# Three fifths of a feed-forward's first layer with the activations stationary and 512 weight columns streaming

## The chip, the cores and the metric

The kernel runs on one core of one Trainium2 chip. The metric is the device time of one execution in microseconds. Before the change three runs took 2414.76, 2416.9 and 2419.35 us, median 2416.9.

## The reference

One block of a transformer on 256 tokens of width 2048, in float32: a feed-forward, a mixer (differential attention and a gated delta rule side by side) and a second feed-forward. Each is modulated by vectors that come from a conditioning vector c (adaLN: shift, scale and gate), and each ends in a residual sum and a layer norm. Cut to what matters here:

```python
def swiglu_ffn(h, w_in, w_out):               # w_in 2048 x 11264, w_out 5632 x 2048
    g, u = jnp.split(h @ w_in, 2, axis=-1)
    return (jax.nn.silu(g) * u) @ w_out

ada = (silu(c) @ w_ada + b_ada).reshape(B, 3, 3, D_MODEL)
shift, scale, gate = ada[:, :, 0, None], ada[:, :, 1, None], ada[:, :, 2, None]
y = swiglu_ffn(x * (1 + scale[:, 0]) + shift[:, 0], w_ffn_in[0], w_ffn_out[0])
x = layer_norm(ALPHA * x + 0.5 * gate[:, 0] * y, ...)
y = hybrid_mixer(x * (1 + scale[:, 1]) + shift[:, 1], ...)
x = layer_norm(ALPHA * x + gate[:, 1] * y, ...)
y = swiglu_ffn(x * (1 + scale[:, 2]) + shift[:, 2], w_ffn_in[1], w_ffn_out[1])
x = layer_norm(ALPHA * x + 0.5 * gate[:, 2] * y, ...)
```

## The kernel before, in words

Products are made to float32 precision in a float32r format: each operand is split into a rounded part hi and a rest lo, and `mm3` (lines 145 to 150) sums three products, hi x hi, hi x lo and lo x hi, into one PSUM bank. Each is one matmul instruction with its own weight load (a 128 x 128 stationary operand) and a moving operand of 256 or 512 columns.

Weights come from DRAM as chunks of 128 x 1024 floats, 512 KB each, in one long `plan` (lines 1464 to 1500) that fixes their order. `weights()` (lines 219 to 231) hands out the next chunk; up to six raw chunks are under way (pool `rawp`, tile `raw`), and up to four are split ahead (pool `wp`, tiles `hi` and `lo`): ACT copies raw to hi, DVE subtracts hi from raw to give lo (POOL does it in a few stretches). DMAs are issued from SP's queue.

There are two ways to use a chunk. `_wstat` (line 274) has the weights stationary: 128 weight columns at a time, with the activations' 256 tokens as the moving operand; the result has features on partitions, tokens along the row. `_xstat` (line 287) has the activations stationary: 128 tokens (t = 0 or 1) by 128 features, with 512 weight columns moving; the result has tokens on partitions. The activations come as hi and lo too: `h` (tiles `h_hi`, `h_lo`, 16 k-tiles of 128 x 256) for a sub-block's input, `hid` for the hidden layer. `h` lies in the pool `pp`, which is opened first, so that `rawp`, `wp` and the pools of each sub-block (`hid` among them) come behind it in SBUF.

A feed-forward has 44 "pairs": 128 gate columns and the 128 up columns that go with them. It runs in two halves (`SIZES`: 28 and 16 pairs in the first feed-forward, 22 and 22 in the last), each with its first layer and then its part of the second layer, since the hidden tiles of all pairs would not fit. In the first layer (lines 791 to 793) each pair is one `_wstat` over 4 chunks, 96 products of 256 columns into one bank; `_ffn_hid_run` (line 737) then makes the hidden tile: Silu on ACT, a product on DVE, and the split into hid hi (ACT) and hid lo (DVE). The first 28 pairs of the whole kernel are another way of this: they wait for the conditioning (tile `mms`, weights `w_first`) and are not touched by the change. The second layer (`_y_blocks`, line 702) is four `_xstat` with hid stationary, one per 512 output columns. The last one of a sub-block works with halves of 256 columns in its last part, so that the layer norm can start early.

At the end of the mixer, `_Next.rest` (line 569) makes the next sub-block's h: PE transposes the normed x (tile `lnt`), DVE applies scale and shift (`hf`), ACT and POOL split it. While these tiles come out, PE already works on the first two pairs of the next stage (tile `pre`).

The order of the instructions on each engine is written out by the kernel itself. `_Kernel` keeps a planned time `k.t` that grows by each product's columns; side work (hidden tiles, adaLN vectors, attention heads) runs as generator threads, and `pump()` after each `mm3` issues the next step of those whose planned time has come. `bank()` gives PSUM banks from a ring of four and waits for the thread that reads the oldest. `k.tr` is a PE transpose (line 158). The adaLN vectors are dot products on DVE (`_ada_dot`, tile `ar`) or, for gates, sums over chunks (tile `acc`) closed by two small PE products (`aps`).

The mixer has one stage with h stationary and 512 columns moving: the attention's values (`dv`, `_xstat` at line 1344, 192 products, tile `mx`). Its other projections are `_wstat`.

Of the kernel before, what the change touches and what calls it, by code (L numbers as in the profile page):

```python
# [8 lines left out]
F32 = mybir.dt.float32  # L9
F32R = mybir.dt.float32r  # L10
I32 = mybir.dt.int32
AF = mybir.ActivationFunctionType
# [6 lines left out]
S = 256  # L19
DFF = 5632  # L20
# [7 lines left out]
NEG = -1.0e30  # L28
BLK = 16
LEVELS = (128 // BLK).bit_length() - 1  # L30
SIZES = {0: (28, 16), 2: (22, 22)}
VISITS = ((0, 2, 0, 28), (2, 2, 0, 28), (4, 4, 0, 28), (8, 4, 0, 12), (8, 8, 12, 28), (12, 4, 0, 12))
SRAW = 4
FIRST_LOADS = (0, 1)
# [22 lines left out]
class _Thread:  # L57
# [3 lines left out]
    def __init__(self, k, gen):  # L61
        self.k, self.gen, self.ready, self.done = k, gen, k.t, False
# [29 lines left out]
class _Kernel:  # L92
# [118 lines left out]
    def hold(self, first, n):  # L211

        u = self.uid()
        bufs = [self.pp.tile([128, KT, S], F32R, tag=f"h_{x}", name=f"held_{x}{u}").rearrange("p a b -> p (a b)")
                for x in ("hi", "lo")]
        for i in range(n):
            self.held[first + i] = [b[:, i * 1024:(i + 1) * 1024] for b in bufs]
# [65 lines left out]
def _tile(part, kt):  # L283
    return part[kt] if isinstance(part, dict) else part[:, kt, :]


def _xstat(k, n, act, done, tail=0):

    pss = [k.bank([128, 512], "mx") for _ in range(2)]
    halves = [(0, 512)]
    pss = [[ps] for ps in pss]
    if tail:
        halves = [(0, 256), (256, 512)]
        pss = [[pss[0][0], pss[1][0]],
               [k.pss.tile([128, 512], F32, tag="sm", name=f"mx{k.uid()}") for _ in range(2)]]

    def part(c, w, j, t, i):  # L300
        kt = 2 * c + j
        act.need(k, kt)
        lo, hi = halves[i]
        sl = slice(j * 512 + lo, j * 512 + hi)
        tk = slice(t * 128, (t + 1) * 128)
        k.mm3(pss[t][i][:, lo:hi], (_tile(act[0], kt)[:, tk], _tile(act[1], kt)[:, tk]), (w[0][:, sl], w[1][:, sl]),
              start=(kt == 0), stop=(kt == 2 * n - 1))
        k.pump()

    more = max(0, tail - WB)  # L310
    if more:
        k.hold(k.nu + n - tail, more)
    for c in range(n - tail):
        w = k.weights()
        for j in range(2):
            for t in range(2):
                for i in range(len(halves)):
                    part(c, w, j, t, i)
    if not tail:
        for t in range(2):  # L320
            k.read(done(t, pss[t][0], 0, 512), 2 - t)
        return
    ws = [k.weights(max(0, i - more)) for i in range(tail)]
    for t in range(2):
        for i, (lo, hi) in enumerate(halves):
            for c in range(n - tail, n):
                for j in range(2):
                    part(c, ws[c - n + tail], j, t, i)
            for _ in done(t, pss[t][i], lo, hi):
                pass  # L330
# [154 lines left out]

def _new_h(k):
    u = k.uid()
    h = _H([k.pp.tile([128, KT, S], F32R, tag=f"h_{x}", name=f"h_{x}{u}") for x in ("hi", "lo")])
    h.ready = 0
    return h  # L490

# [53 lines left out]
class _Next:  # L545


    def __init__(self, k, idx, prep):
        self.k, self.idx, self.prep = k, idx, prep

    def step(self, stage, ada, ln):
        k = self.k
# [16 lines left out]
    def rest(self, ln):  # L569
        k, A, B = self.k, self.A, self.B  # L570
        h = _new_h(k)
        x, lnp = k.x, k.lnp
        k.xd = k.drp.tile([128, 2, D], F32, tag="xd", name=f"xd{self.idx}")

        def turn(ps, g, t):
            for j in range(2):
                f = 2 * g + j
                k.tr(ps[:, j, t * 128:(t + 1) * 128], x[t][:, f * 128:(f + 1) * 128])

        def bank(g):  # L580
            ps = k.pss.tile([128, 2, 256], F32, tag="sm", name=f"lnt{k.uid()}")
            turn(ps, g, 0)
            return ps

        ln.norm(0, 2)
        ln.norm(0, 3)
        pss = [bank(g) for g in range(3)]
        ln.factors(1)
        ln.norm(1, 0)
        k.pool_lo = 0  # L590
        def run():
            for g in range(8):
                ps = pss.pop(0)
                turn(ps, g, 1)
                for i in range(2):
                    f = 2 * g + i
                    _h_tile(k, lnp, h, f, ps[:, i, :], A[:, f:f + 1], B[:, f:f + 1])
                if g in (0, 2, 4):
                    ln.norm(1, 1 + g // 2)
                h.ready = 2 * g + 2  # L600
                h.when[2 * g] = h.when[2 * g + 1] = k.chain
                yield 0.0
                if g < 5:
                    pss.append(bank(g + 3))
            for t in range(2):
                k.nc.sync.dma_start(k.xd[:, t, :], x[t])

        th = k.spawn(run())
        th.step()
        acts = [h, h]  # L610
        pre = [k.bank([128, 2, S], "pre") for _ in range(2)]
        for c in range(4):
            for ps in pre:
                _products(k, ps, k.weights(), 4 * c, 4, acts, c == 0, c == 3)
        k.wait(lambda: th.done)
        return h, pre
# [140 lines left out]
    k.V.tensor_tensor(hid[1][j], hf, hid[0][j].bitcast(F32), ALU.subtract)  # L757


def _ffn(k, a, h, sub, items, interval, start, pre, finish, tail):  # L760

    tc = k.tc
    acts = [h, h]
    ln = _Ln(k)
    with ExitStack() as fs:
        k.hp = hp = fs.enter_context(tc.tile_pool(name=f"hid{sub}", bufs=1))
        for half, size in enumerate(SIZES[sub]):
            hid = _H([{}, {}])
            hid.ready = size
            j0 = 0  # L770
            if half == 0:

                def side():
                    k.pss = k.pss or k.ctx.enter_context(tc.tile_pool(name="pss", bufs=4, space=PSUM))
                    ada = _Ada(k, a, fs.enter_context(tc.tile_pool(name=f"ada{sub}", bufs=1)), items, interval)
                    k.lnp = fs.enter_context(tc.tile_pool(name=f"ln{sub}", bufs=1))
                    k.spawn(_load_x(k, a, k.lnp, k.lnp, ("x0", "x1"), *((1, 40.0, X_PACE) if sub else (None, 0.0, 3.0))))
                    return ada

                if start is not None:  # L780
                    j0 = size
                    ada = start(h, hid, side)
                    k.spawn(_rel_bias(k, a))
                    k.spawn(_lambda(k, a))
                    k.spawn(k.consts())
                else:
                    j0 = len(pre)
                    for j in range(j0):
                        _ffn_hid(k, pre[j], hid, j, back=j0 - j)
                    ada = side()  # L790
            for j in range(j0, size):
                ps = _wstat(k, 4, acts)
                _ffn_hid(k, ps, hid, j)
            res = _y_blocks(k, size // 2, hid, ada, sub, half == 0, ln if half else None, finish, tail)
        return res

# [636 lines left out]
def tile_hybrid_block(ctx: ExitStack, tc: tile.TileContext, names, aps):  # L1433
# [6 lines left out]
    k.pp = pp = ctx.enter_context(tc.tile_pool(name="pp", bufs=1))  # L1440
    k.rawp = ctx.enter_context(tc.tile_pool(name="rawp", bufs=RAWB))
    k.wp = ctx.enter_context(tc.tile_pool(name="wp", bufs=WB))
    k.smallp = ctx.enter_context(tc.tile_pool(name="smallp", bufs=2))
    k.drp = ctx.enter_context(tc.tile_pool(name="drp", bufs=1, space=DRAM))

# [11 lines left out]
    k.ones = pp.tile([128, 128], F32R, tag="ones", name="ones")  # L1457
    k.V.tensor_copy(k.ones, one)
    k.V.tensor_scalar(k.badaT[:, 0, 1, :], k.badaT[:, 0, 1, :], 1.0, None, ALU.add)
    k.eps = pp.tile([128, 1], F32, tag="eps", name="eps")  # L1460
    k.V.memset(k.eps, LN_EPS)
    k.xd = a["x"]

# [2 lines left out]
    plan += [a["w_first"][i] for i in range(4 * SIZES[0][0])]  # L1466
    for sub in range(2):
        j0 = 0
        if sub == 1:
            plan += [a["w_ffn_in"][sub, j, c] for c in range(4) for j in range(2)]  # L1470
            j0 = 2
        for half, size in enumerate(SIZES[2 * sub]):
            if sub or half:
                plan += [a["w_ffn_in"][sub, j, c] for j in range(j0, NPAIR if half else size) for c in range(4)]
            j0 = SIZES[2 * sub][0]
            plan += [a[f"w_ffn_out{sub}{half}"][n, c] for n in range(4) for c in range(size // 2)]
        if sub == 0:
            n0 = len(plan)
# [92 lines left out]
        d = {**ada.dst, **k.more.dst}  # L1571
        return _affine(k, 2, 1, d[(2, 0)], d[(2, 1)])

    h, pre = _ffn(k, a, h, 0, FFN_ADA, FFN_PACE, start, None, _Next(k, 0, prep0), TAIL)
    h, pre = _mixer(k, a, h, pre, lambda pool: _Ada(k, a, pool, TAIL_ADA, TAIL_PACE), _Next(k, 1, prep1))
    last = _Last(k, a, out)
    k.spawn(last.load())
    _ffn(k, a, h, 2, [(2, 2)], 6.0, None, pre, last, LAST_TAIL)
# [37 lines left out]
def _layout(inputs, np):  # L1616
# [32 lines left out]
    r["ln_gT"] = r["ln_g"].reshape(3, KT, 128).transpose(2, 0, 1)  # L1649
    r["ln_bT"] = r["ln_b"].reshape(3, KT, 128).transpose(2, 0, 1)  # L1650
    wi = g["w_ffn_in"].reshape(2, D, 2 * DFF)
    wi = [pair(w[:, :DFF], w[:, DFF:]) for w in wi]
    r["w_ffn_in"] = np.stack([chunks_w(w, 2) for w in wi])
    first = []
    for kt0, n, ja, jb in VISITS:
        m, q = min(n, 4), max(1, 4 // n)
# [49 lines left out]
```

## Time and profile before

| | |
|---|---|
| median of three runs | 2416.9 us |
| the profiled execution | 2417.43 us, of which the span is 2415.6 |
| PE (matmul) busy | 2331.5 us, 97% |
| DVE busy | 1708.3 us, 71% |
| ACT busy | 1036.6 us, 43% |
| POOL busy | 323.1 us, 13% |
| DMA | 582.06 MB, mean 241 GB/s |
| granted TensorE clock, mean | 0.984 of full speed |

PE's matmuls are pipelined: a row's duration is longer than the distance from one start to the next, so a busy share of 97% does not say how fast the products follow each other. That is to be had from the number of products in a stretch that holds nothing else. PEld is the weight load, which runs beside the products. Where a helper issues all of an engine's work, every row has the helper's line (L88), and the tiles' names tell the groups apart: out<-in.

### The profile page before, as it was taken

How to read it: one execution, taken by the hardware profiler on the slowest of the kernel's cores; microseconds unless marked ns; L12 is line 12 of the kernel's file. 1: busy time of each engine (PE TensorE's matmuls, PEld its weight loads, DVE VectorE, ACT ScalarE, POOL GpSimd, SP SyncE). 2: the span in 40 equal slices, each digit the busy share in tenths (PEclk: the TensorE clock that was granted, in tenths of full speed). 3: DMA queues.
4: the chain of work that ended last, by engine and by line, in shares of the span. 5: the costliest groups of instructions: out<-in, count | busy, mean ns of one | idle time of the engine just before them, and what ended most of it. 6: DMA issues, size and time to landing. Idle time of an engine off the chain costs nothing.

```text
span 2415.6 us, 42349 instructions
## 1 busy us (share of the span) xinstructions
PE 2331.5 (97%) x16989; PEld 2214.6 (92%) x16989; DVE 1708.3 (71%) x2538; ACT 1036.6 (43%) x1420; POOL 323.1 (13%) x218
## 2 busy tenths in 40 slices
PE   6999999999999899999999999999999999999997
PEld 6999997889998879998999999988999989999987
DVE  4767888787765687869887887876787555444456
ACT  4434444444444444444444344435434434444432
POOL 5884000000002210000000300022040000000001
PEclk8999999999999999999999999999999999999999
DMA  9997878898875565544547888876888555555553
GB/s 363 333 329 289 296 248 275 317 336 301 300 262 191 183 206 193 168 166 153 168 160 262 299 308 291 290 261 214 300 311 261 188 192 192 183 183 183 186 191 106
DMA packets 166381, 582.06 MB, mean 241 GB/s; under 512 B 19820, under 2 KB 22812, under 8 KB 165416
## 3 DMA queue, kind: packets, MB, share of 16 engines
q1 hardware_dynamic: 166184, 579.36, 68.9%
q8 instruction: 133, 2.18, 0.4%
q14 instruction: 64, 0.52, 0.1%
HBM read 572.98 MB, written 7.88 MB: 240 GB/s over the span
## 4 chain that ended last, share of the span: by engine, by line
PE 87%; DVE 7%; issue 2%; ACT 1%; DMA 1%; POOL 1%; DVEq 0%; SPq 0%; ACTq 0%; POOLq 0%
PE mm L147 15%; PE mm L148 15%; PE mm L149 15%; PE mx L149 8%; PE mx L147 8%; PE mx L148 8%; PE mms L148 4%; PE mms L147 4%; PE mms L149 4%; DVE lo L88 2%; DVE acc L88 1%; PE UY L153 1%; DVE x L88 1%; ACT hi L88 1%; PE pre L148 1%
## 5 line engine op out<-in xcount | busy, mean ns | idle before, releaser
L88 ACT ACTIVATE hi<-raw 128x1024 fp32r<-128x1024 f32 x769 | 811.9, 1059 | 995.9 <-PE mm L148 413.4
L88 DVE TENSOR_TENSOR lo<-raw,hi 128x1024 fp32r<-128x1024 f32 x690 | 855.2, 1245 | 524.6 <-ACT hi L88 516.8
L147 PE MATMUL mm<-h_hi,hi 128*128 128x256 f32 x3072 | 878.1, 286 | 0.0
L149 PE MATMUL mm<-h_hi,lo 128*128 128x256 f32 x3072 | 868.0, 283 | 3.6 <-DVE lo L88 3.6
L148 PE MATMUL mm<-h_lo,hi 128*128 128x256 f32 x3072 | 869.6, 283 | 0.0
L149 PEld LDWEIGHTS mm<-h_hi,lo 128*128 128x128 f32 x3072 | 583.3, 190 | 4.3 <-DVE lo L88 4.3
L147 PEld LDWEIGHTS mm<-h_hi,hi 128*128 128x128 f32 x3072 | 581.6, 189 | 1.9 <-issue 1.6
L148 PEld LDWEIGHTS mm<-h_lo,hi 128*128 128x128 f32 x3072 | 581.6, 189 | 1.0 <-issue 0.6
L88 POOL TENSOR_TENSOR lo<-raw,hi 128x1024 fp32r<-128x1024 f32 x79 | 189.9, 2412 | 793.4 <-ACT hi L88 793.4
L147 PE MATMUL mx<-hi,hid 128*128 128x512 f32 (+1 forms) x772 | 285.3, 370 | 1.4 <-ACT hi L88 1.4
L148 PE MATMUL mx<-lo,hid 128*128 128x512 f32 (+1 forms) x772 | 285.3, 370 | 0.8 <-DVE lo L88 0.8
L149 PE MATMUL mx<-hi,hid 128*128 128x512 f32 (+1 forms) x772 | 285.1, 369 | 0.0
L147 PE MATMUL mms<-h_hi,hi 128*128 128x256 f32 x896 | 256.2, 286 | 9.9 <-ACT hi L88 5.7
L148 PE MATMUL mms<-h_lo,hi 128*128 128x256 f32 x896 | 255.4, 285 | 3.7 <-POOL h_lo L88 3.7
L149 PE MATMUL mms<-h_hi,lo 128*128 128x256 f32 x896 | 254.3, 284 | 1.6 <-POOL lo L88 1.6
L147 PEld LDWEIGHTS mms<-h_hi,hi 128*128 128x128 f32 x896 | 170.5, 190 | 10.6 <-ACT hi L88 5.8
L148 PEld LDWEIGHTS mms<-h_lo,hi 128*128 128x128 f32 x896 | 171.3, 191 | 4.3 <-POOL h_lo L88 4.2
L149 PEld LDWEIGHTS mms<-h_hi,lo 128*128 128x128 f32 x896 | 172.1, 192 | 1.9 <-POOL lo L88 1.9
L147 PEld LDWEIGHTS mx<-hi,hid 128*128 128x128 f32 x772 | 145.5, 189 | 26.7 <-ACT hi L88 1.9
L148 PEld LDWEIGHTS mx<-lo,hid 128*128 128x128 f32 x772 | 145.5, 188 | 25.9 <-DVE lo L88 1.4
L149 PEld LDWEIGHTS mx<-hi,hid 128*128 128x128 f32 x772 | 145.5, 188 | 24.4
L88 DVE SCALAR_TENSOR_TENSOR acc<-ar,cs,acc 128x512 f32<-128x512 f32 x180 | 147.7, 821 | 6.3 <-DMA ar<-in_w_gate_dram 2.9
(295 smaller groups left out, 2436.7 us busy)
## 6 DMA issues: line engine op xcount, KB each, us to landing
raw<-in_w_ffn_in_dram SPq DMA_DIRECT2D x240, 512.0 KB, 4.4
raw<-in_w_ffn_out_dram SPq DMA_DIRECT2D x176, 512.0 KB, 4.1
raw<-in_w_first_dram SPq DMA_DIRECT2D x112, 512.0 KB, 5.1
ar<-in_w_gate_dram SPq DMA_DIRECT2D x96, 512.0 KB, 4.9
ar<-in_w_ada_dram SPq DMA_DIRECT2D x96, 512.0 KB, 5.4
sar<-in_w_ada_dram SPq DMA_DIRECT2D x64, 512.0 KB, 4.7
raw<-in_w_gab_dram SPq DMA_DIRECT2D x64, 512.0 KB, 4.7
raw<-in_w_kq_dram SPq DMA_DIRECT2D x32, 512.0 KB, 3.2
```

Of the source, the lines that this page charges most:

```text
L88: return f(*args, **kw)
L147: mm(ps, lhsT=lhs[0], rhs=rhs[0], start=start, stop=False, skip_group_check=True)
L148: mm(ps, lhsT=lhs[0], rhs=rhs[1], start=False, stop=False, skip_group_check=True)
L149: mm(ps, lhsT=lhs[1], rhs=rhs[0], start=False, stop=stop, skip_group_check=True)
L153: self.nc.tensor.matmul(ps, lhsT=lhsT, rhs=rhs, start=start, stop=stop, skip_group_check=True)
```

## The change

60 of the 88 pairs, the second half of the first feed-forward (16) and all of the last one (44), are made in blocks of four by `_ffn_block`: first the four pairs' 512 gate columns with `_xstat` (h stationary, 8 chunks, 96 products of 512 columns into two banks, one per 128 tokens), then their 512 up columns likewise into two other banks. ACT takes Silu of each gate bank into `sg0` and `sg1`, DVE multiplies by the up bank in place. As tokens now lie on partitions, a thread `turn` transposes the 2 x 4 tiles on PE into two PSUM tiles (`hT`), four transposes each, and ACT and DVE split from there into hid hi and lo. The turn starts 2 us of planned time behind DVE's planned end, and the next block's gate may be read only when it is done. `w_ffn_in` is laid out as `_xstat` wants it, and the plan asks for a block's 8 gate chunks and then its 8 up chunks. The last feed-forward's halves become 24 and 20 pairs. At its start, PE works on the first block's gate columns while h comes out (`wide`), k-tile by k-tile for both token halves, instead of on two pairs. h moves from `pp` to a pool of its own, `htp`, opened behind `rawp` and `wp`; `eps`, a tile of one float per partition that stood ahead of h, becomes 16 floats wide.

```diff
-SIZES = {0: (28, 16), 2: (22, 22)}
+SIZES = {0: (28, 16), 2: (24, 20)}
...
-    h = _H([k.pp.tile([128, KT, S], F32R, tag=f"h_{x}", name=f"h_{x}{u}") for x in ("hi", "lo")])
+    h = _H([k.htp.tile([128, KT, S], F32R, tag=f"h_{x}", name=f"h_{x}{u}") for x in ("hi", "lo")])
...
+def _xprod(k, ps, w, act, kt, j, t, lo, hi, last):
+
+    act.need(k, kt)
+    sl = slice(j * 512 + lo, j * 512 + hi)
+    tk = slice(t * 128, (t + 1) * 128)
+    k.mm3(ps[:, lo:hi], (_tile(act[0], kt)[:, tk], _tile(act[1], kt)[:, tk]), (w[0][:, sl], w[1][:, sl]),
+          start=(kt == 0), stop=(kt == last))
+    k.pump()
...
+        if self.wide:
+            pre = [k.bank([128, 512], "pre") for _ in range(2)]
+            for c in range(8):
+                w = k.weights()
+                for j in range(2):
+                    for t in range(2):
+                        _xprod(k, pre[t], w, h, 2 * c + j, j, t, 0, 512, KT - 1)
+            k.wait(lambda: th.done)
+            return h, pre
...
+def _ffn_block(k, h, hid, b, before, pre):
+    sg = {}
+
+    def gate(t, ps, lo, hi):
+        yield 0.2
+        while not all(th.done for th in before):
+            yield 0.3
+        sg[t] = k.hp.tile([128, 512], F32, tag=f"sg{t}", name=f"sg{k.uid()}")
+        k.A.activation(sg[t], ps, AF.Silu)
+
+    def up(t, ps, lo, hi):
+        yield 0.2
+        k.V.tensor_tensor(sg[t], sg[t], ps, ALU.mult)
+
+    def turn(ups):
+        while not all(th.done for th in ups):
+            yield 0.3
+        yield max(0.0, k.V.t - k.t) + 2.0
+        for g in range(2):
+            ps = k.pss.tile([128, 2, S], F32, tag="sm", name=f"hT{k.uid()}")
+            for q in range(2):
+                for t in range(2):
+                    f = 2 * g + q
+                    k.tr(ps[:, q, t * 128:(t + 1) * 128], sg[t][:, f * 128:(f + 1) * 128])
+            yield
+            js = [4 * b + 2 * g + q for q in range(2)]
+            for q, j in enumerate(js):
+                both = k.hp.tile([128, 2, S], F32R, tag=f"hid{j}", name=f"hid{k.uid()}")
+                hid[0][j], hid[1][j] = both[:, 0, :], both[:, 1, :]
+                k.A.activation(hid[0][j], ps[:, q, :], AF.Copy)
+            yield
+            for q, j in enumerate(js):
+                k.V.tensor_tensor(hid[1][j], ps[:, q, :], hid[0][j].bitcast(F32), ALU.subtract)
+
+    if pre is None:
+        _xstat(k, KT // 2, h, gate)
+    else:
+        for t in range(2):
+            k.read(gate(t, pre[t], 0, 512), 2 - t)
+    _xstat(k, KT // 2, h, up)
+    th = k.spawn(turn(list(k.users[-2:])))
+    for i in range(4):
+        hid.job(4 * b + i, th)
+    return th
...
-                    j0 = len(pre)
-                    for j in range(j0):
-                        _ffn_hid(k, pre[j], hid, j, back=j0 - j)
                     ada = side()
-            for j in range(j0, size):
-                ps = _wstat(k, 4, acts)
-                _ffn_hid(k, ps, hid, j)
+            turned = []
+            for b in range(b0, size // 4):
+                turned = [_ffn_block(k, h, hid, b, turned, None if b or half else pre)]
...
     k.rawp = ctx.enter_context(tc.tile_pool(name="rawp", bufs=RAWB))
     k.wp = ctx.enter_context(tc.tile_pool(name="wp", bufs=WB))
+    k.htp = ctx.enter_context(tc.tile_pool(name="htp", bufs=1))
...
-    k.eps = pp.tile([128, 1], F32, tag="eps", name="eps")
+    k.eps = pp.tile([128, 16], F32, tag="eps", name="eps")[:, 0:1]
...
-                plan += [a["w_ffn_in"][sub, j, c] for j in range(j0, NPAIR if half else size) for c in range(4)]
+                plan += [a[f"w_ffn_in{sub}"][i, b, c] for b in range(j0, j0 + size // 4) for i in range(2)
+                         for c in range(KT // 2)]
```

## Rows read from the trace of the kernel before

**Rows 1.** The page's part 1: busy time, share of the span, instructions.
```profile
PE 2331.5 (97%) x16989; PEld 2214.6 (92%) x16989; DVE 1708.3 (71%) x2538; ACT 1036.6 (43%) x1420; POOL 323.1 (13%) x218
```
**Rows 2.** The page's part 4: the chain that ended last, by engine, by line.
```profile
PE 87%; DVE 7%; issue 2%; ACT 1%; DMA 1%; POOL 1%; DVEq 0%; SPq 0%; ACTq 0%; POOLq 0%
PE mm L147 15%; PE mm L148 15%; PE mm L149 15%; PE mx L149 8%; PE mx L147 8%; PE mx L148 8%; PE mms L148 4%; PE mms L147 4%; PE mms L149 4%; DVE lo L88 2%; DVE acc L88 1%; PE UY L153 1%; DVE x L88 1%; ACT hi L88 1%; PE pre L148 1%
```
**Rows 3.** Busy time by windows: first-layer stages (16 and 22 pairs), then a second layer.
```profile
core 0: us, PE busy (x) PEld busy (x) DVE busy (x) ACT busy (x) POOL busy (x), PEclk, DMA share, GB/s
520.40:704.70 184.30, 184.30 (x1538) 184.30 (x1537) 140.71 (x181) 78.61 (x95) 0.00 (x0) 1.00 0.88 305
...
2025.30:2278.80 253.50, 253.50 (x2114) 253.46 (x2113) 124.38 (x134) 105.43 (x130) 0.00 (x0) 1.00 0.53 183
...
1905.60:2025.30 119.70, 119.70 (x530) 99.13 (x529) 62.10 (x58) 47.27 (x46) 0.00 (x0) 1.00 0.57 193
```
**Rows 4.** Tile mx: weight loads and products, duration min/median/max, stationary hid and h.
```profile
L148 PEld LDWEIGHTS mx<-lo,hid x772: 186/188/192, 360.8 to 2399.9; 128*128 128x128 f32 x193
L148 PE MATMUL mx<-lo,hid x772: 282/389/506, 361.0 to 2400.0; 128*128 128x512 f32 x157, 128*128 128x256 f32 x36
...
L147 PE MATMUL mx<-hi,h_hi x64: 391/398/741, 848.5 to 902.4; 128*128 128x512 f32 x64
L148 PEld LDWEIGHTS mx<-lo,h_hi x64: 187/188/192, 848.5 to 902.4; 128*128 128x128 f32 x64
L148 PE MATMUL mx<-lo,h_hi x64: 392/397/400, 848.8 to 902.6; 128*128 128x512 f32 x64
```
**Rows 5.** PE's timeline, dv products: first and last of 20 (start, duration in us).
```profile
883.01 0.40 PE L148 MATMUL mx<-lo,h_hi 128*128 128x512 f32 x1
...
887.47 0.40 PE L149 MATMUL mx<-hi,h_lo 128*128 128x512 f32 x1
```
**Rows 6.** PE's timeline: four transposes among 256-column and among 512-column products.
```profile
968.49 0.60 PE L158 MATMUL oT<-ident,kn 128*128 128x128 f32 x4
968.85 0.36 PE L147 MATMUL mm<-h_hi,hi 128*128 128x256 f32 x1
969.05 0.28 PE L148 MATMUL mm<-h_lo,hi 128*128 128x256 f32 x1
...
876.35 0.60 PE L158 MATMUL knT<-ident,kn 128*128 128x128 f32 x4
876.70 0.48 PE L147 MATMUL mx<-hi,h_hi 128*128 128x512 f32 x1
877.02 0.40 PE L148 MATMUL mx<-lo,h_hi 128*128 128x512 f32 x1
```
**Rows 7.** Groups by tile, 520 to 705 us: busy us, mean ns | idle before.
```profile
L88 DVE TENSOR_TENSOR lo<-raw,hi 128x1024 fp32r<-128x1024 f32 x65 | 79.6, 1226 | 43.6 <-ACT hi L88 41.4 <-DMA raw<-in_w_ffn_in_dram 1.5
L88 ACT ACTIVATE hi<-raw 128x1024 fp32r<-128x1024 f32 x65 | 69.0, 1061 | 107.3 <-PE mm L148 87.9 <-issue 14.1 <-DVE ada L88 1.8
L88 DVE CUSTOM_DVE_ANT_0 ar<-ar,crow,tmp 128x1024 f32<-128x1024 f32 x21 | 26.9, 1280 | 0.0
...
L88 DVE TENSOR_TENSOR hid<-hidf,hid 128x256 fp32r<-128x256 f32 x15 | 6.3, 420 | 0.0
L88 DVE TENSOR_TENSOR hidf<-sg,mm 128x256 f32<-128x256 f32 x15 | 6.2, 415 | 0.5 <-ACT sg L88 0.5
L88 ACT ACTIVATE hid<-hidf 128x256 fp32r<-128x256 f32 x15 | 6.1, 409 | 0.0
L88 ACT ACTIVATE sg<-mm 128x256 f32<-128x256 f32 x15 | 5.5, 367 | 0.0
```
**Rows 8.** Groups by tile, 2025 to 2279 us: DVE with 512 columns of PSUM.
```profile
L88 DVE SCALAR_TENSOR_TENSOR res<-mx,gate 128x512 f32<-128x512 f32 x2 | 1.4, 684 | 0.0
```
**Rows 9.** Who waited for whom, 2025 to 2279 us: us, times, longest.
```profile
DVE lo L88 <- ACT hi L88: 130.1, 88, 1.7
ACT hi L88 <- PE mm L148: 115.1, 67, 1.8
```
**Rows 10.** Busy time by windows: the start of the last feed-forward.
```profile
1636.90:1643.00 6.10, 5.48 (x23) 4.92 (x24) 4.74 (x7) 3.56 (x6) 2.85 (x4) 0.50 0.37 103
...
1636.90:1668.00 31.10, 29.37 (x216) 28.43 (x217) 19.51 (x26) 15.36 (x24) 12.40 (x17) 0.89 0.60 203
1668.00:1905.60 237.60, 234.23 (x1930) 233.35 (x1929) 171.60 (x190) 103.26 (x131) 26.38 (x16) 0.99 0.81 275
```
**Rows 11.** The timeline there: POOL.
```profile
1641.81 8.83 POOL L88 TENSOR_TENSOR h_lo<-hf,h_hi 128x256 fp32r<-128x256 f32 x12 [3.20 <-ACT h_hi L88]
```
**Rows 12.** Busy time by windows: the first feed-forward's first stage.
```profile
60.00:200.00 140.00, 140.00 (x1169) 139.98 (x1168) 96.08 (x141) 57.62 (x65) 117.63 (x56) 1.00 0.92 332
```
**Rows 13.** Groups by line and form: 512-column products with hid and mg stationary.
```profile
L148 PE MATMUL mx<-lo,hid 128*128 128x512 f32 x628 | 244.6, 389 | 0.8 <-DVE lo L88 0.8
...
L147 PE MATMUL mx<-hi,mgh 128*128 128x512 f32 x96 | 37.4, 389 | 0.0
```
**Rows 14.** Groups by line and form, 850 to 903 us: a transpose.
```profile
L158 PE MATMUL knT<-ident,kn 128*128 128x128 f32 x4 | 0.6, 273 | 0.0
```

More of the change, by code (lines that the diff above doesn't have):

```diff
@@ L213, in hold @@
         u = self.uid()
-        bufs = [self.pp.tile([128, KT, S], F32R, tag=f"h_{x}", name=f"held_{x}{u}").rearrange("p a b -> p (a b)")
+        bufs = [self.htp.tile([128, KT, S], F32R, tag=f"h_{x}", name=f"held_{x}{u}").rearrange("p a b -> p (a b)")
                 for x in ("hi", "lo")]
@@ L300, in part @@
     def part(c, w, j, t, i):
-        kt = 2 * c + j
-        act.need(k, kt)
         lo, hi = halves[i]
[L304 to L308, printed above, removed]
+        _xprod(k, pss[t][i], w, act, 2 * c + j, j, t, lo, hi, 2 * n - 1)
     more = max(0, tail - WB)
@@ L545, with __init__ @@
 class _Next:
-    def __init__(self, k, idx, prep):
-        self.k, self.idx, self.prep = k, idx, prep
+    def __init__(self, k, idx, prep, wide):
+        self.k, self.idx, self.prep, self.wide = k, idx, prep, wide
     def step(self, stage, ada, ln):
@@ L757, in _ffn_hid_run @@
     k.V.tensor_tensor(hid[1][j], hf, hid[0][j].bitcast(F32), ALU.subtract)
+def _ffn_block(k, h, hid, b, before, pre):
[38 more added lines that the diff above has]
+    return th
 def _ffn(k, a, h, sub, items, interval, start, pre, finish, tail):
     tc = k.tc
-    acts = [h, h]
     ln = _Ln(k)
@@ L769, in _ffn @@
             hid.ready = size
-            j0 = 0
+            b0 = 0
             if half == 0:
@@ L780, in _ffn @@
                 if start is not None:
-                    j0 = size
+                    b0 = size // 4
                     ada = start(h, hid, side)
@@ L1468, in tile_hybrid_block @@
         j0 = 0
-        if sub == 1:
-            plan += [a["w_ffn_in"][sub, j, c] for c in range(4) for j in range(2)]
-            j0 = 2
         for half, size in enumerate(SIZES[2 * sub]):
             if sub or half:
-                plan += [a["w_ffn_in"][sub, j, c] for j in range(j0, NPAIR if half else size) for c in range(4)]
-            j0 = SIZES[2 * sub][0]
+                plan += [a[f"w_ffn_in{sub}"][i, b, c] for b in range(j0, j0 + size // 4) for i in range(2)
+                         for c in range(KT // 2)]
+                j0 += size // 4
             plan += [a[f"w_ffn_out{sub}{half}"][n, c] for n in range(4) for c in range(size // 2)]
@@ L1572, in prep1 @@
         return _affine(k, 2, 1, d[(2, 0)], d[(2, 1)])
-    h, pre = _ffn(k, a, h, 0, FFN_ADA, FFN_PACE, start, None, _Next(k, 0, prep0), TAIL)
-    h, pre = _mixer(k, a, h, pre, lambda pool: _Ada(k, a, pool, TAIL_ADA, TAIL_PACE), _Next(k, 1, prep1))
+    h, pre = _ffn(k, a, h, 0, FFN_ADA, FFN_PACE, start, None, _Next(k, 0, prep0, False), TAIL)
+    h, pre = _mixer(k, a, h, pre, lambda pool: _Ada(k, a, pool, TAIL_ADA, TAIL_PACE), _Next(k, 1, prep1, True))
     last = _Last(k, a, out)
@@ L1651, in _layout @@
     wi = g["w_ffn_in"].reshape(2, D, 2 * DFF)
+    for sub in range(2):
+        j0 = (NPAIR if sub else SIZES[0][1]) * 128
+        r[f"w_ffn_in{sub}"] = np.stack([chunks_x(wi[sub][:, DFF * i - j0:DFF * i]) for i in (1, 2)])
     wi = [pair(w[:, :DFF], w[:, DFF:]) for w in wi]
-    r["w_ffn_in"] = np.stack([chunks_w(w, 2) for w in wi])
     first = []
```

## The prediction

> **What bounds the kernel now.** I read the page's busy times first: TensorE (PE) is busy for 2331.5 us, 97% of the span, DVE 71%, ACT 43% [rows 1]. The chain of waits says the same from the other end: 87% of the chain that ended last is PE, and its largest lines are the three products of mm3 (15% each on tile mm, 8% each on mx) [rows 2]. So the time is the sum of the starts of PE's products, and an edit counts by what it does to the interval from one product to the next. That interval is not in a row's duration (283 or 389 ns), because products overlap; it is read from windows that hold nothing else. Of three such stages two are first-layer stages with 256-column products, without one idle stretch of PE: 2025.3 to 2278.8 us is 22 pairs x 96 = 2112 products in 253.5 us, 120.0 ns each; 520.4 to 704.7 us is 16 pairs, 1536 products in 184.3 us, again 120.0 ns. The third is a second-layer stage with 512 columns: 4 blocks x 11 chunks x 12 = 528 products in 119.7 us, 226.7 ns (the x counts take in two at the edges) [rows 3]. Two products of 256 columns take 240.0 ns, one of 512 takes 226.7: 13.3 ns less for the same arithmetic. At 2.4 GHz 512 columns are 213.3 ns, so each product carries some 13.3 ns beside its columns.
>
> **The change part by part.**
>
> *Products.* 60 of the 88 pairs go from 96 products of 256 columns to 48 of 512. Out: 60 x 96 = 5760 x 120.0 ns = 691.2 us. In: 15 blocks x 192 = 2880 x 226.7 ns = 652.9 us. **-38.3 us**, if h as stationary part runs as hid does.
> By the Trainium skill ("TensorE: Matmul & The Clock Gate", "Back-to-back issue gap") a product adds about 2.5 ns to its columns at full clock; an estimate from that is 109.2 ns for 256 and 215.8 for 512 columns, so 2.6 ns gained per pair of products, 7.5 us in all, less than the transposes below cost. The trace disagrees: 120.0 and 226.7 ns, 13.3 in both.
>
> *Where h lies.* One stage of before already has h stationary, the mixer's dv: there a 512-column product shows a median of 397 or 398 ns where hid shows 389, with the weight loads alike (188 ns) [rows 4]. The clean stretch from 883.01 to 887.47 us holds 19 intervals, 234.7 ns each [rows 5], 8.0 more than hid's. Two things differ: h's tiles lie in pool pp, ahead of the raw and weight parts, and 32 bytes past a multiple of 64 (from the sizes in the code, each tile rounded up to 32 bytes), while weight parts and hid lie on multiples of 64. The change puts h behind the weight parts, where hid lies, and the widened eps then shifts weight parts, h and hid alike by 32 bytes; they keep their places to each other. Bounds for the new products: 226.7 (hid) and 234.7 ns (dv), 23.0 us apart over 2880. I take 226.7, since h then stands to the weights as hid does. The dv products then gain too: 192 x 8.0 = **-1.5 us**.
>
> *Transposes.* The hidden block now comes out with tokens on partitions and must be turned: 15 blocks x 8 = 120 transposes, in 30 groups of four. Four transposes in a row at 968.49 us put the second product behind them at 969.05; without them it would start 0.12 after 968.49, so they cost 0.44 us. Between 512-column products, at 876.35, the second starts at 877.02 instead of 0.23 after: 0.44 again [rows 6]. 30 x 0.44 = **+13.2 us**.
>
> *ACT and DVE.* Per four pairs before: ACT 4 x (367 + 409) ns = 3.1 us, DVE 4 x (415 + 420) = 3.3 us [rows 7]. After: two Silu and two products 512 wide, four copies and four subtractions of 256; at 684 ns for a 512-wide DVE operation on PSUM [rows 8] DVE has 2 x 684 + 4 x 420 = 3.0 us, ACT about as much as before. The weight split is the same per chunk, 1061 on ACT and 1226 ns on DVE, and a chunk's products last 12 x 226.7 = 2.72 instead of 24 x 120.0 = 2.88 us. Cost 0: ACT's waits before its splits are mostly for PE to free a weight part (115.1 us in the stage of 22 pairs) [rows 9], so these engines have slack. What can be late is the turn: its transposes stand in PE's queue with the next gate's products behind them, and wait for DVE's product of Silu and up. The code puts them 2 us behind DVE's planned time. On time costs 0; late by one adaLN dot product ahead of them in DVE's queue (1280 ns [rows 7]) costs 15 x 1.28 = 19 us. I take **+1**, near the lower end, since the stage of 22 pairs has no such dot product. The last block's turn has at least 12 k-tiles of the second layer ahead of it, 12 x 6 x 0.227 = 16 us.
>
> *Start of the last feed-forward.* The first two pairs now wait for h tile by tile: 1636.9 to 1668.0 us is 31.1 us for 192 products (23.0 us) and 24 transposes (2.6), so 5.5 us are lost, at a granted clock of 0.50 in the first 6.1 us [rows 10]. POOL makes the h_lo tiles, 12 in 8.83 us, 0.74 us each [rows 11]. Before, pair 0 asks for four k-tiles at 6 x 120 ns each, as fast as they come, and a turn follows every 0.36 us of products. After, a k-tile feeds 6 x 226.7 ns = 1.36 us of work, and PE does twice the work between turns. Between 0 and 3 us are gained, as the slow clock lasts or not; I take **-2**.
>
> *Transfers.* The same bytes come in less time. The 16-pair stage becomes 4 blocks of 192 x 226.7 ns = 43.5 us and two groups, 0.88: 177.6 us, so its 305 GB/s [rows 3] become 305 x 184.3 / 177.6 = 317. From 60 to 200 us the queue moved 332 GB/s with PE never idle [rows 12], so this costs 0; if 305 were all that the queue can do beside this work, the stage would keep its 184.3 us and 6.7 us of the gain go.
> *The rest.* 24 + 20 pairs instead of 22 + 22 move 24 products of 256 columns to 12 of 512: -0.2 us.
>
> **Sum.** -38.3 - 1.5 + 13.2 + 1 - 2 - 0.2 = -27.8 us. The profiled execution took 2417.4 us, 1.8 over its span; 2417.4 - 27.8 = 2389.6. It lies 0.5 over the median of the three runs, so I predict 2389.
>
> **The rivals.**
> 1. *h stays slow as the stationary part* (234.7 ns wherever it lies): the 23.0 us and the 1.5 are not gained, -3.3: 2414. For it: it is the only row with h stationary. Against: hid, in the same role, does not show it [rows 4].
> 2. *Slower than before: the 32-byte shift slows every 512-column stream.* If what costs dv its 8.0 ns is the place past a multiple of 64 and not the place relative to the weights, hid and mg get it too: 3 x 628 + 3 x 96 = 2172 products [rows 13] x 8.0 = 17.4 us on top of rival 1, +14.1: 2431. It decides from 5.2 ns more on all 5052 streams (26.3 / 5052). Against: 256-column products with h as the moving part keep their mean of 120.0 ns at that place [rows 3].
> 3. *The turns cost more*: late by 1.28 us each (19 us, above), or a group costs its transposes' durations, 4 x 273 = 1.09 us [rows 14], so 30 x 0.65 = 19.5 us more. Either gives 2408. Against the second: the four at 876.35 took 0.60 us together [rows 6].
> The Trainium skill (same page, "Part 4: PE-mode transpose") gives about 275 ns for one in a kernel; an estimate from it is 120 x 275 = 33 us. The trace has that as duration, not as interval.
> 4. *Only about 2.6 ns are gained per pair of products*, so the transposes outweigh them: 7.5 instead of 38.3 us, +3.0: 2420. The intervals speak against it; it is the result of the first page above.
>
> **How the numbers follow.** My forecast 0.58, rival 1 0.17, rival 2 0.12, rival 3 0.10, rival 4 and anything else 0.03. The forecast's own range is 2380 (3 us at the start, no late turn, and the 237.6 - 1920 x 0.12 = 7.2 us that the next 20 pairs lose between 1668.0 and 1905.6 us, where PE waits for DVE's sums [rows 10], lost no more) to 2402 (two thirds of the turns late). The range for 8 in 10 reaches on to rivals 3 and 1, 2381 to 2416, and leaves out rivals 2 and 4. This kernel's measurement tells about 0.2%, 4.8 us, from no change. Faster than 2412.1 are the forecast, rival 3 and a third of rival 1: 0.74. The same: the rest of rival 1 and a little of the others, 0.12. Slower: rival 2 and part of 4, 0.14.
>
> **What would show it.** Right: first-layer stages of 44.4 us for four pairs (192 x 226.7 ns + 0.88) instead of 46.1; products mx<-h at a duration of 389 ns, mx<-hid unchanged at 389; 120 transposes whose groups move the next products by 0.44 us; the stage of 16 pairs at about 178 us, PE never idle in it. Wrong: mx<-h near 397 ns (rival 1), mx<-hid near 397 too (rival 2), PE idle before tile hT with DVE as releaser (rival 3). The prediction is wrong as a whole if the first-layer stages lose less than 10 us.

## The result, and the profile after

The changed kernel took 2391.68 us, median of four runs (2389.68 to 2396.75), against 2416.53 us before: a ratio of 0.9899, 95% interval 0.9887 to 0.9910. The prediction was 2389. The change touches 60 of the 88 pairs, 68%, which is nearer two thirds than the title's three fifths. The profiled execution took 2389.68 us with a span of 2387.9, 27.7 us less than the span before.

The page's parts 1 and 4 of the changed kernel, as [rows 1, 2]:

```profile
PE 2305.5 (97%) x14217; PEld 2071.9 (87%) x14217; DVE 1707.0 (71%) x2508; ACT 1033.1 (43%) x1390; POOL 329.1 (14%) x218
...
PE 86%; DVE 7%; issue 2%; DMA 1%; POOL 1%; ACT 1%; SPq 0%; DVEq 0%; ACTq 0%; POOLq 0%
PE mx L148 17%; PE mx L147 17%; PE mx L149 17%; PE mm L147 6%; PE mm L148 6%; PE mm L149 6%; PE mms L148 4%; PE mms L149 4%; PE mms L147 4%; DVE lo L88 2%; DVE acc L88 1%; PE UY L153 1%; DVE x L88 1%; ACT hi L88 1%; PE hT L158 1%
```

PE has 16989 - 14217 = 2772 instructions fewer: 2880 + 12 products are gone (each time two of 256 columns became one of 512; the 12 are at the kernel's end) and 120 transposes have come. PE is still busy for 97% of the span and still makes up most of the chain; the load has moved from tile mm to tile mx.

Busy time by windows of the changed kernel, as [rows 3]: the stages of 16 and of 20 pairs, and, as in [rows 10], the first layer of the last feed-forward's first half (24 pairs) from its first product on:

```profile
520.40:697.40 177.00, 177.00 (x794) 146.53 (x793) 138.59 (x170) 76.76 (x85) 0.00 (x0) 1.00 0.90 316
...
2039.90:2261.40 221.50, 221.50 (x994) 183.37 (x993) 110.62 (x108) 94.54 (x106) 0.00 (x0) 1.00 0.60 190
...
1631.40:1908.40 277.00, 274.38 (x1225) 225.54 (x1226) 198.60 (x212) 126.47 (x153) 42.42 (x33) 0.99 0.79 273
```

The 16 pairs take 177.0 instead of 184.3 us, 20 pairs 221.5 us where 22 took 253.5: 44.3 us for four instead of 46.1. The turn of each stage's last block stands behind these windows; with its 0.88 us (below) the 20 pairs take 44.5 for four. PE is busy throughout both, and the queue moves 316 GB/s in the first without holding it up.

Tile mx of the changed kernel, as [rows 4] (duration min/median/max):

```profile
L148 PE MATMUL mx<-lo,h_hi x992: 387/389/628, 520.6 to 2260.9; 128*128 128x512 f32 x199
L148 PE MATMUL mx<-lo,hid x768: 282/389/504, 361.0 to 2372.5; 128*128 128x512 f32 x158, 128*128 128x256 f32 x34
```

With h stationary the median is now hid's, 389 ns, where before it was 397. The turns are shown next: by tile hT with what held PE up before them (us, times), and in PE's timeline (start, duration), as [rows 6]:

```profile
L158 PE MATMUL hT<-ident,sg x120: 270/272/328, 570.1 to 2270.3; 128*128 128x128 f32 x120
...
  DVE sg L88: 0.3, 1
```
```profile
2089.56 0.60 PE L158 MATMUL hT<-ident,sg 128*128 128x128 f32 x4
2089.91 0.48 PE L147 MATMUL mx<-hi,h_hi 128*128 128x512 f32 x1
2090.23 0.40 PE L148 MATMUL mx<-lo,h_hi 128*128 128x512 f32 x1
```

A group of four costs 2090.23 - 2089.56 - 0.23 = 0.44 us. Taken over more of the products around them, by their starts, the 30 groups cost 0.46 or 0.47 us each, but for one at 0.61, so 14.1 in all. That one is the only group that DVE held up: its weight load waited 0.3 us for tile sg.

Where the 27.7 us came from, by the starts of the stages in the two traces: the 16 pairs -7.3; the second layer and norm behind them +0.9 (the last turn of the 16 pairs stands there); the mixer up to the last feed-forward +0.9; the last feed-forward from its first product to the end, 778.7 to 756.5 us, -22.2.

### The profile page after: what moved, and what is told of

Its sections match the earlier page's. It is cut to its first block, busy times and chain, and to the rows that moved or that the text cites. A ratio compares the mean times of both kernels' runs of the same rounds, so it can differ in the third digit from the quotient of the medians.

```text
span 2387.9 us, 36796 instructions
## 1 busy us (share of the span) xinstructions
PE 2305.5 (97%) x14217; PEld 2071.9 (87%) x14217; DVE 1707.0 (71%) x2508; ACT 1033.1 (43%) x1390; POOL 329.1 (14%) x218
## 4 chain that ended last, share of the span: by engine, by line
PE 86%; DVE 7%; issue 2%; DMA 1%; POOL 1%; ACT 1%; SPq 0%; DVEq 0%; ACTq 0%; POOLq 0%
PE mx L148 17%; PE mx L147 17%; PE mx L149 17%; PE mm L147 6%; PE mm L148 6%; PE mm L149 6%; PE mms L148 4%; PE mms L149 4%; PE mms L147 4%; DVE lo L88 2%; DVE acc L88 1%; PE UY L153 1%; DVE x L88 1%; ACT hi L88 1%; PE hT L158 1%
## 5 line engine op out<-in xcount | busy, mean ns | idle before, releaser
L147 PE MATMUL mx<-hi,h_hi 128*128 128x512 f32 x992 | 389.7, 393 | 0.0
L149 PE MATMUL mx<-hi,h_lo 128*128 128x512 f32 x992 | 387.2, 390 | 0.0
L148 PE MATMUL mx<-lo,h_hi 128*128 128x512 f32 x992 | 387.0, 390 | 0.0
L147 PE MATMUL mm<-h_hi,hi 128*128 128x256 f32 x1216 | 354.4, 291 | 0.0
L149 PE MATMUL mm<-h_hi,lo 128*128 128x256 f32 x1216 | 346.5, 285 | 3.4 <-DVE lo L88 3.4
L148 PE MATMUL mm<-h_lo,hi 128*128 128x256 f32 x1216 | 346.4, 285 | 0.0
L88 POOL TENSOR_TENSOR lo<-raw,hi 128x1024 fp32r<-128x1024 f32 x79 | 190.2, 2415 | 788.0 <-ACT hi L88 788.0
L149 PEld LDWEIGHTS mm<-h_hi,lo 128*128 128x128 f32 x1216 | 235.2, 193 | 3.9 <-DVE lo L88 3.9
L147 PEld LDWEIGHTS mm<-h_hi,hi 128*128 128x128 f32 x1216 | 235.7, 194 | 1.7 <-issue 1.6
L148 PEld LDWEIGHTS mm<-h_lo,hi 128*128 128x128 f32 x1216 | 235.7, 194 | 0.7 <-issue 0.6
L147 PEld LDWEIGHTS mx<-hi,h_hi 128*128 128x128 f32 x992 | 186.7, 188 | 38.2 <-issue 0.2
```

Source lines behind the costliest of these rows:

```text
L88: return f(*args, **kw)
L147: mm(ps, lhsT=lhs[0], rhs=rhs[0], start=start, stop=False, skip_group_check=True)
L148: mm(ps, lhsT=lhs[0], rhs=rhs[1], start=False, stop=False, skip_group_check=True)
L149: mm(ps, lhsT=lhs[1], rhs=rhs[0], start=False, stop=stop, skip_group_check=True)
```

## The experiments

They ask three things: what about h's place decides the 8 ns by which dv's products were slower, what the transposes cost, and what the gain is worth beside the placement. Every part's address is worked out from the order and widths of the tiles in the code, each rounded up to 32 bytes; no trace shows it. D stands for the distance from the weight parts to h, modulo 256 bytes; that of hid is 0 in all of them but h_behind_off32, where it is 32 too. "Interval" is the mean from one start to the next where PE does not wait (under 245 ns for 512, under 135 ns for 256 columns), worked out from the start times of each trace. The column headed mm has h as the moving part. Ratios are to runs of the kernel before made beside each kernel, with medians of 2416.5 to 2418.3 us.

| kernel | D, h's place | 512, h: duration, interval | 512, hid: interval | 256, mm: interval | median us |
|---|---|---|---|---|---|
| before | 96, ahead | 397, 234 | 227 | 120 | 2416.5 |
| changed | 0, behind | 389, 227.1 | 226.9 | 119.8 | 2391.7 |
| h_ahead_off32 | 96, ahead | 397, 234.2 | 226.9 | 119.9 | 2413.2 |
| h_ahead_aligned | 64, ahead | 394, 233.3 | 226.9 | 117.7 | 2405.2 |
| h_ahead_mod128 | 128, ahead | 393, 232.7 | 226.9 | 118.8 | 2403.2 |
| h_ahead_mod256 | 0, ahead | 389, 227.0 | 226.8 | 119.8 | 2394.9 |
| h_behind_off32 | 32, behind | 395, 233.2 | 233.3 | 116.8 | 2408.6 |
| h_behind_no_pad | 0, behind | 389, 227.1 | 226.8 | 119.8 | 2392.7 |

**h_ahead_off32: h back where it was.** Here and below the buffers of `hold()`, which share h's tiles, move with h; this is not shown.

```diff
-    h = _H([k.htp.tile([128, KT, S], F32R, ...
+    h = _H([k.pp.tile([128, KT, S], F32R, ...
...
-    k.eps = pp.tile([128, 16], F32, tag="eps", name="eps")[:, 0:1]
+    k.eps = pp.tile([128, 1], F32, tag="eps", name="eps")
```

> The changed kernel with h back in pp ahead of the raw and weight parts and eps one float wide again: h lies 32 bytes past a multiple of 64, weight parts and hid on multiples of 64, as in the kernel before. Theory A (a 512-column product is slowed when stationary and moving part differ by 32 bytes modulo 64): products with h stationary take 234.7 ns instead of 226.7, a duration of 397 instead of 389, so 2880 x 8.0 = 23 us more: about 2415 us. Theory B (h must lie behind the weight parts): the same, 2415. If the place of h costs nothing: 2392, durations of 389.

2413.22 us, ratio to before 0.9986 (0.9976 to 0.9995). Tile mx of this run:

```profile
L148 PE MATMUL mx<-lo,h_hi x992: 392/397/628, 520.6 to 2285.3; 128*128 128x512 f32 x199
```

Without its placement the change gains almost nothing: the 2880 new products are 7.2 ns slower each, 21 us, and the time is rival 1's 2414 within 1 us. Theories A and B are not told apart by this.

**h_ahead_aligned: ahead, but on a multiple of 64 like the weights.**

```diff
-    h = _H([k.htp.tile([128, KT, S], F32R, ...
+    h = _H([k.pp.tile([128, KT, S], F32R, ...
...
-    k.lam = k.pp.tile([128, 1], F32, tag="lam", name="lam")
+    k.lam = k.pp.tile([128, 16], F32, tag="lam", name="lam")[:, 0:1]
```

> h in pp ahead of the weight parts, but eps and lam 16 floats wide, so that h, weight parts and hid all lie on multiples of 64. Theory A (difference of 32 bytes modulo 64): products with h stationary at 226.7 ns (duration 389), about 2392 us. Theory B (h must lie behind the weight parts): 234.7 ns (397), about 2415 us.

2405.17 us. The products with h are slow:

```profile
L148 PE MATMUL mx<-lo,h_hi x992: 388/394/628, 515.6 to 2277.1; 128*128 128x512 f32 x199
```

Theory A in its first form (a difference of 32 modulo 64) falls. The time lies under theory B's 2415 by two things that neither expected. The 512-column products with h took 233.3 ns, not 234.7. And the 256-column products with h as the moving part took 117.7 instead of 120 ns: the first stage was over at 355.5 us instead of 360.8.

**h_behind_off32: behind, and 32 bytes off.**

```diff
-    k.eps = pp.tile([128, 16], F32, tag="eps", name="eps")[:, 0:1]
+    k.eps = k.htp.tile([128, 8], F32, tag="eps", name="eps")[:, 0:1]
```

> h behind the weight parts, with eps as a tile of 32 bytes between them: weight parts 32 bytes past a multiple of 64, h, hid and mg on multiples of 64. Theory A (difference of 32 bytes modulo 64): every 512-column product is slow, with h, hid and mg: (2880 + 2172) x 8.0 = 40 us more, about 2432 us, durations of 397 everywhere. Theory B (h must lie behind the weight parts): as the changed kernel, about 2392 us, durations of 389.

2408.62 us, between the two. Every 512-column product is slow, hid's too, so theory B falls, as h and hid both lie behind the weight parts:

```profile
L148 PE MATMUL mx<-lo,h_hi x992: 392/395/628, 517.7 to 2278.5; 128*128 128x512 f32 x199
L148 PE MATMUL mx<-lo,hid x768: 277/395/633, 352.8 to 2392.0; 128*128 128x512 f32 x158, 128*128 128x256 f32 x34
```

The 256-column products at 116.8 ns gave back part of the 40 us that theory A charged. Against the changed kernel, the first stage was over at 352.6 instead of 360.8 us, and the mixer behind dv took 630.9 instead of 638.6 us.

**h_behind_no_pad: the changed kernel without the wider eps.**

```diff
-    k.eps = pp.tile([128, 16], F32, tag="eps", name="eps")[:, 0:1]
+    k.eps = pp.tile([128, 1], F32, tag="eps", name="eps")
```

> The changed kernel with eps one float wide: h behind the weight parts, and weight parts, h and hid all on multiples of 64 instead of 32 bytes past them. Theory A and theory B: no difference, 2392 us within 0.2%, durations of 389. If the shift of all parts by 32 bytes is what makes the products fast, durations of 397 with h and about 2415 us.

2392.65 us and 389 ns: no difference. The widening does nothing, as everything is shifted by it alike. Rival 2 is out with this: the products are as fast with all parts 32 bytes past a multiple of 64 as with all on one. The changed kernel itself says so too, as hid's 389 ns stayed under the shift.

**h_ahead_mod128 and h_ahead_mod256: which distance counts.** Both are h_ahead_aligned with lam 64 and 32 floats wide, D = 128 and 0.

> The changed kernel with h back in pp ahead of the weight parts, eps 16 and lam 64 floats wide, so that h and the weight parts differ by a multiple of 128 bytes (by 128 modulo 256). Theory A2 (stationary and moving part must differ by a multiple of 128 bytes, wherever they lie; the three slow placements differed by 96, 64 and 32): products with h stationary at 226.7 ns, duration 389, about 2392 us. Theory B (h must lie behind the weight parts) or a period of 256 bytes or more: 233 to 234 ns, about 2405 to 2415 us.

2403.17 us, and 393 ns: A2's period of 128 bytes falls.

```profile
L148 PE MATMUL mx<-lo,h_hi x992: 387/393/628, 517.4 to 2274.9; 128*128 128x512 f32 x199
```

> The changed kernel with h in pp ahead of the weight parts, eps 16 and lam 32 floats wide, so that stationary and moving parts all differ by multiples of 256 bytes. Theory A3 (the two reads lock, 226.7 ns for 512 and 120.0 ns for 256 columns, when their places differ by a multiple of 256 bytes, wherever they lie; the slow placements differed by 32, 64, 96 and 128 modulo 256): 226.7 ns, about 2392 us. Theory B (h must lie behind the weight parts): 232 to 234 ns, about 2403 to 2413 us.

2394.86 us. h lies ahead of the weights and is as fast as behind them:

```profile
L148 PE MATMUL mx<-lo,h_hi x992: 387/389/628, 519.3 to 2265.8; 128*128 128x512 f32 x199
```

Theory A3's condition stands: five distances were run, and only 0 modulo 256 gives 227 ns, on either side. A period of 512 is out by hid, which by the tiles' sizes lies at 256 modulo 512 and takes 227 ns. That the two reads "lock" is a name for it; no run shows what happens inside.

**transposes_twice: each transpose of the turns made two times.**

```diff
-                    k.tr(ps[:, q, t * 128:(t + 1) * 128], sg[t][:, f * 128:(f + 1) * 128])
+                    for _ in range(2):
+                        k.tr(ps[:, q, t * 128:(t + 1) * 128], sg[t][:, f * 128:(f + 1) * 128])
```

> The changed kernel with each of the 120 transposes of the turns made twice, into the same place. By the intervals (0.109 us from one to the next in a row of them): 120 x 0.109 = 13.1 us more, about 2405 us. By their durations (272 ns, rival 3): 120 x 0.272 = 32.6 us more, about 2424 us. If the turns stand beside PE's stream: 2392 us.

2402.27 us, 10.6 more than the changed kernel (span 12.1 more): 0.09 to 0.10 us for each of 120, near the interval of 0.109 and far from the duration of 0.272. The starts around the groups say it more closely: every group of eight costs 0.89 us where four cost 0.46 or 0.47, so 0.105 for each.

**before_layout_only: the placement without the change.**

```diff
-    h = _H([k.pp.tile([128, KT, S], F32R, ...
+    h = _H([k.htp.tile([128, KT, S], F32R, ...
...
-    k.eps = pp.tile([128, 1], F32, tag="eps", name="eps")
+    k.eps = pp.tile([128, 16], F32, tag="eps", name="eps")[:, 0:1]
```

> The kernel before with the change's placement alone: h in htp behind the weight parts and eps 16 floats wide, all first-layer pairs still with 256 columns. Theory A2: all parts differ by multiples of 128 bytes, 256-column products at a steady 120.0 ns, the dv products at 226.7 instead of 234.7 (1.5 us): 2415 to 2417 us, no difference that can be told. If the placement itself gives the gain: towards 2392 us.

2415.81 us, ratio 0.9993 (0.9984 to 1.0003): nothing. The change's gain needs both its parts: streaming alone gave 0.14%, placement alone 0.07%, both together 1.0%.

**before_h_16_48_32 and before_h_y_off32: the kernel before, with h placed for 256 columns.**

```diff
-    h = _H([k.pp.tile([128, KT, S], F32R, ...
+    o = k.hoff.pop(0)             # floats: 4, 12, 8 in the first run; 8, 8, 8 in the second
+    h = _H([k.htp.tile([128, KT * S + 32], F32R, ...)[:, o:o + KT * S]
+            .rearrange("p (a b) -> p a b", a=KT) for x in ("hi", "lo")])
```

In the second run the tiles are 64 floats longer, so that h_hi and h_lo both lie 32 bytes off (32 floats put h_lo 128 bytes further), and ya and yb are slices like these.

> The kernel before, all first-layer pairs with 256 columns, h behind the weight parts in a tile 128 bytes longer, of which h is a slice: 16 bytes past a multiple of 128 in the first feed-forward, 48 in the mixer, 32 in the last feed-forward, with weight parts, hid and mg on multiples of 128. In the run with h 32 bytes off, 256-column products took 116.8 ns instead of 120.0. Theory A2 in full (no lock between the two reads: 512 columns slower, 256 columns faster): about 117 ns for tiles mms, mm and pre, mx with hid still 226.7, 13000 x 3.1 = 40 us less than before, about 2376 us, below the changed kernel. If only the changed kernel's order of work made them faster: 120.0 ns and 2416 us. Whether 16 and 48 bytes do as 32 does is open: each of them that does not leaves about 8 (16) or 11 us (48) of the 40.

2395.54 us: at all three offsets the products take less than 120.0 ns on average (117.8 in the first feed-forward and the last 22 pairs, 116.7 in the mixer), but 22.7 us came instead of 40. By the intervals the products with h account for some 30 of the 40. The mixer behind dv, at 633.0 instead of 638.1 us, kept under half of its share of some 12; that it also waits for other work is argued, not shown.

> The kernel before, all first-layer pairs with 256 columns, h behind the weight parts; h, ya and yb lie 32 bytes past a multiple of 256, weight parts, hid and mg on multiples of 256. From the 116.8 ns at 32 bytes and the 226.7 at 0: tiles mms, mm and pre at 116.8 ns, mx with hid and mg at 226.7; the products with h and y are some 13000 x 3.1 = 40 us shorter, of which the run with 16, 48 and 32 bytes showed about four fifths (29 us of products gave 23): about 2385 us, 2376 if all of it counts. If h's exact place does not matter beyond not being a multiple: 2395.

2384.19 us, ratio 0.9862 (0.9845 to 0.9878). The stage of 22 pairs in this run:

```profile
2001.30:2247.70 246.40, 246.40 (x2113) 246.38 (x2112) 124.31 (x134) 105.45 (x130) 0.00 (x0) 1.00 0.60 189
```

246.4 us for 2112 products are 116.7 ns each, 11.20 us a pair; the changed kernel's 20 pairs in 221.5 us are 11.08, or 11.12 with the last turn.

**mixed_off32_x1: the better of both for each stage.**

```diff
-                turned = [_ffn_block(k, h, hid, b, turned, None if b or half else pre)]
+                if sub == 0:
+                    for j in range(4 * b, 4 * b + 4):
+                        _ffn_hid(k, _wstat(k, 4, [h, h]), hid, j)
+                else:
+                    turned = [_ffn_block(k, h, hid, b, turned, None if b or half else pre)]
```

Not shown is the placement: h lies 32 bytes off in the first feed-forward and the mixer (ya and yb too) and at a distance of 0 modulo 256 in the last feed-forward.

> Both kernels put together: the first feed-forward and the mixer with 256-column products and h, ya and yb 32 bytes past a multiple of 256; the last feed-forward as in the changed kernel, 512 columns streaming over h on a multiple of 256. Against the kernel of the run before, 44 pairs take 2112 x 226.7 ns and 22 groups of transposes at 0.44 us, 488.5 us, instead of 4224 x 116.8 = 493.4: 5 us less than that kernel, about 2380 us, and 10 to 17 us under the changed kernel. If the mixer is set by other waits, 2385.

2381.89 us, ratio to before 0.9854 (0.9840 to 0.9869): the fastest of all, some 10 us under the changed kernel. Its interval overlaps that of before_h_y_off32, so the 2.3 us between those two are not told apart: on top of the better placement no run shows a gain from the wide products.

## Why the prediction was right

**Products: right.** 226.7 ns was taken over 234.7 because h would stand to the weights as hid does. The starts in the changed kernel give 227.1 ns, 0.4 more than the sum has, or 1.1 us over 2880 products. The upper bound was mis-sized: the 19 intervals at 234.7 are not the whole of dv, whose mean is 234.2, so the bounds lie 21 and not 23 us apart. The reason was right in kind: what counts is the distance between the two parts. But it was named too coarsely, as a place behind the weights and modulo 64; the runs put 256 in its place. A distance of 64 or 128 bytes meets the prediction's modulo 64 and gave 233 ns, and a place behind the weights alone did not help either (h_behind_off32). That the new place was also 0 modulo 256 was not worked out ahead; that much is luck. By h's distance alone the change is worth 25 us or 3.

**Where h lies, dv: the -1.5 us did not come.** Away from the wait below its products did run at 227 ns, but the stage took 54.8 instead of 54.6 us. The rows are the stage before, the stage after, and 3.4 us within it:

```profile
848.50:903.10 54.60, 52.57 (x248) 42.03 (x247) 43.05 (x92) 24.72 (x43) 9.59 (x19) 1.00 0.58 194
...
842.30:897.10 54.80, 52.95 (x247) 42.98 (x246) 43.41 (x92) 24.81 (x43) 10.36 (x20) 0.97 0.60 197
...
851.70:855.10 3.40, 3.40 (x10) 2.63 (x9) 3.35 (x8) 1.69 (x2) 0.00 (x0) 0.50 0.14 12
```

PE waits there, at the gates' small product (tile pG), for DVE's tile g. Who waited for whom in it, before and after:

```profile
PEld pG L153 <- DVE g L88: 1.4, 1, 1.4
...
PEld pG L153 <- DVE g L88: 2.3, 1, 2.3
```

The wait is 0.9 us longer, and behind it the granted clock falls to 0.50, 1.2 GHz, for 3.4 us; before, it stayed at 1.00 behind the shorter wait. At 0.50 the products start 0.43 instead of 0.23 us apart, which costs some 1.6 us. Wait and clock together take the 1.4 us that the products gave, and a little more. The prediction counted this stage by its products alone. PE reaches the wait only 0.2 us earlier in the stage (6.6 instead of 6.8 us). DVE's g comes 0.7 us later in it (8.8 instead of 8.1), behind a wait of DVE for POOL; why is open. In the other runs with the changed kernel's order and D = 0 the stage took 55.9 or 56.0 us.

**Transposes: right**, +13.2 predicted, 13 to 14 found (30 groups of 0.44 to 0.47). The Trainium skill's 275 ns for one ("TensorE: Matmul & The Clock Gate", "Part 4: PE-mode transpose") is near the duration here, 272; doubling them shows that the time goes by the interval.

**ACT, DVE and the turns: right at the lower end.** One late group, by 0.14 us in PE's starts, instead of the +1.

**Start of the last feed-forward: right in size.** From the first product on tile pre to the first that is on another, it took 31.1 us before and 28.0 after; 1.3 of the 3.1 belong to the products' sum, 1.8 are gained against the 2 predicted. The pairs behind it (20 before, 22 after) lost 4.8 us (249.0 less 1056 x 227.1 ns and ten groups of 0.44) where before they lost 7.2. The three kernels with D = 0 (changed, h_behind_no_pad, h_ahead_mod256) spread over 277.0 to 281.1 us from the first product of this half to its second layer, so these 2.4 us may well be chance.

**Transfers: right**: 316 GB/s against the 317 worked out, and PE never idle.

**The sum** is -27.8, and the profiled execution gave -27.7. Misses cancel in it: dv's 1.5 that did not come, 0.9 more in the mixer and 1.1 from the products' 0.4 ns on the one side, no late turns (1) and the 2.4 on the other. So the agreement to 0.1 us is luck. It is also that of one execution, the fastest of four that spread over 7 us; the medians differ by 24.9, 2.9 less than the sum. What the runs bear out is the mechanism and its size: the products give 37 of the 38 us, and the transposes take 13 to 14 of them.

**The rivals.** Rival 1's price was right and its condition (slow wherever h lies) wrong: h_ahead_off32 is that kernel, at 2413 for 2414. Rival 2 fell with the changed kernel's hid and with h_behind_no_pad. Rival 3 fell with transposes_twice and tile hT. Rival 4 is out by the intervals of every run: 13.3 ns per pair of products, not 2.6, at a distance of 0 modulo 256; though the last section finds 6.7 where each width has its own best place.

## What to carry to other kernels

When one product with many columns replaces two with fewer, read the interval of both from a window of starts, with the operands in the places that they will have; a duration or a busy share shows neither. Before restructuring, move the operands: here 32 bytes between stationary and moving part, for h, ya and yb, gave the kernel before 33 us, more than the 25 of the rewrite with its transposes. At that distance 256-column products gain (120.0 to 116.7 ns) and 512-column ones lose (226.7 to 233.2). A pad that shifts everything alike changes nothing.

## What the runs showed of the hardware

With both parts at a distance of 0 modulo 256 bytes, 256-column products follow each other every 120.0 ns and 512-column ones every 226.7 to 227.1, in the changed kernel with a spread (standard deviation) of under 2 ns. At 32, 64 and 128 bytes, with h or hid, 512-column products take 232.7 to 233.3 ns and 256-column ones 116.7 to 118.8; at 96, 234.2 and 119.9. So a restructuring from 256 to 512 columns is worth 13.3 ns per pair of products on one placement, and 2 x 116.7 - 226.7 = 6.7 ns with the best placement of each.

The Trainium skill ("TensorE: Matmul & The Clock Gate", "Part 2: What happens when you issue a matmul") says that PE reads stationary and moving operand through two independent ports, and that loading the next weights takes no read bandwidth of SBUF from the running product. For these float32r products the runs do not bear out that independence: the same loads and products at another distance from each other move the interval by up to 7 ns. What makes it so, no run here shows. Of the distances only 0, 32, 64, 96 and 128 bytes were run with h_hi and h_lo alike; 16 and 48 bytes were run only in a kernel whose h_lo lies 128 bytes further than its h_hi, 48 there with dv's 512 columns too (230.5 ns).
